# Layer kernel of a two-layer diffusion backbone: modulation loads issued from the GpSimd queue, and the last down weights of each FFN split once for two token blocks

## The chip, the cores and the metric

The kernel runs on one core of a Trainium2 chip. The metric is the device time of one execution in microseconds (us). Before the change it is 2483.01 us, the median of three runs (2481.47 to 2483.67).

Engines are named as in the profile: PE (TensorE matmuls; PEld is its weight load), DVE (VectorE), ACT (ScalarE), POOL (GpSimd) and SP (SyncE, which here only issues transfers). Each engine works through its own instructions in the order in which they stand. DMA transfers are issued by instructions on such a queue: "SPq" is the SP queue, and POOL's transfers stand in the same queue as POOL's arithmetic.

## The reference, cut to what matters

Two layers work on 512 latent tokens and 256 context tokens, all in float32:

```python
sh1, sc1, g1, sh2, sc2, g2 = split(silu(c) @ w_ada[l] + b_ada[l], 6)     # the modulation, once per layer
h = rmsnorm(x, norm1_g[l]) * (1 + sc1) + sh1
x = x + g1 * hybrid_mixer(h, hc, ...)     # three token mixers, merged by gates, then w_out
h = rmsnorm(x, norm2_g[l]) * (1 + sc2) + sh2
x = x + g2 * ((silu(h @ w_gate) * (h @ w_up)) @ w_down)
```

The context tokens go through the same in layer 0 (modulated by a constant vector), and only serve as keys and values in layer 1. w_ada has 1024 x 6144 elements a layer, w_gate and w_up 1024 x 2816, w_down 2816 x 1024.

## The kernel before, in words

Activations lie transposed, with features on the 128 partitions and tokens along the free dimension (768 tokens in layer 0, 512 in layer 1). Every dense product is done to float32 accuracy by three matmuls: a weight tile and an activation are each split into a high and a low part, and high x high, high x low and low x high are summed in PSUM.

**Weights.** `dense` (L303) computes one tile of 128 output features. `load_w` (L290) first loads the weight tile from HBM through the SP queue into one of three raw buffers `wr` (L283), copies it into the high part `wh` on ACT (L295), and subtracts to get the low part `wl` on DVE (L296); `wh` and `wl` have two buffers each. The matmuls of `dense` are at L313. A list `self.early` holds weights that were split ahead; `dense` takes from it first. In layer 0, most of the FFN's gate and up products use a seven-product scheme instead (`seven`, L419): POOL forms sums of weight blocks there (L435, four adds for each product of two tiles), which are split by ACT and DVE (L760, L761) and used by the matmuls at L413.

**Modulation.** The vector product with w_ada is not done on PE, apart from the first four units: its rows are multiplied in on DVE, a row of 128 x 512 weights at a time. `ada_load` (L545) loads one such row block `wra` (256 KB) into a pool with a single buffer, `aw`. `ada_step` (L549) multiplies it by a scalar per partition and adds it to an accumulator `acc` (L531 on DVE; the first row of each unit on ACT, L529). Where the modulation of latent and context tokens is needed (nb = 2), each row costs two such operations, otherwise one. `fill` (L609) does one step and issues the next load. `fill` is called after the tiles of the branch merge in `layer`, after the down tiles of the FFN pieces, and after each seven-product in layer 0. Since there is one buffer, the load of a row can't start before the operation on the row ahead of it has ended, and that operation stands in DVE's order between the weight splits (L296) and the other work. 136 row blocks go through `ada_load`; 24 more are loaded in pairs by `fill_unit` (L620) through the raw buffers.

**The FFN's last piece.** The FFN is cut into pieces of D_FF (`FF_PIECES`); each piece is followed by its part of the down product over eight tiles of output features, added to the residual stream X (`add_res`, L808). In the last piece the down product is done in two token blocks one after the other (layer 0: 512 latent and 256 context tokens; layer 1: 256 and 256), so that the norm of the first block (`settle`) can go on beside the second. Each block calls `dense` for all eight tiles, so each down tile of the last piece is loaded and split twice: 128 x 512 elements a tile in layer 0 (four blocks of D_FF), 128 x 768 in layer 1 (six).

**Pages.** Other tiles lie in 27 pages of two halves, taken (`pair`, `single`) and freed in the order of the program; a new tile in a page waits for the readers of the old one.

**Order.** The code is written in one order, and a scheduler places the instructions of each engine when the program is built. In layer 0's merge it stands up to three modulation rows to a tile of the merge, in layer 1's two. POOL's other work there is the sum `macc` (L1326), one add per merge tile, and the reload of X from its spill in HBM (L778).

Of the kernel before, what the change touches and what calls it, by code (L numbers as in the profile page):

```python
# [10 lines left out]
F32R = mybir.dt.float32r  # L11
# [5 lines left out]
P = 128  # L17
# [89 lines left out]
class Builder:  # L107
# [178 lines left out]
    def stationary(self, kt):  # L286
        return [pool.tile([P, KD, P], F32R, tag=tag, name=self.nm(tag))[:, 0:kt, :]
                for pool, tag in ((self.wh, "wh"), (self.wl, "wl"))]

    def load_w(self, wap, kt):  # L290
        nc = self.nc
        raw = self.load_raw(wap, kt)
        hi, lo = self.stationary(kt)
        r, h, o = (t.rearrange("p k c -> p (k c)") for t in (raw, hi, lo))
        nc.scalar.activation(out=h, in_=r, func=AF.Copy)  # L295
        nc.vector.tensor_tensor(out=o, in0=r, in1=h.bitcast(F32), op=ALU.subtract)  # L296
        return hi, lo
# [246 lines left out]

    def ada_load(self):  # L545
        self.ada_raw = self.aw.tile([P, 1, 512], F32, tag="aw", name=self.nm("wra"))
        self.nc.sync.dma_start(out=self.ada_raw, in_=self.ada_rows_of(1))

    def ada_step(self, w):  # L549
        state, l, units, nb, i, k = self.ada_queue.pop(0)  # L550
# [704 lines left out]
    def layer(self, l):  # L1255
        nc, a = self.nc, self.a
# [4 lines left out]
        def wcol(c0):  # L1261
            return win[:, c0:c0 + P]
# [40 lines left out]
        for bi, (idx, src) in enumerate(((2, cc), (0, at), (1, o))):  # L1303
# [5 lines left out]
            for m in range(KD):  # L1309
                pg = self.dense(wcol(OFF_GT + idx * D + m * P), act, [(0, tt)])  # L1310
# [35 lines left out]
        for bi, blk in enumerate(blocks):  # L1346
            for m in range(KD):
                ps = self.dense(a["w_out"][l][:, m * P:(m + 1) * P], mact, [blk[1:]])
# [8 lines left out]
        f0 = 0  # L1357
# [3 lines left out]
        for pi, n in enumerate(pieces):  # L1361
            last = pi == len(pieces) - 1
            gu, guheld = [], []
            for i in range(min(n, max(0, plain - f0))):
                c0 = (f0 + i) * P
                early = pi == 0 and i == 0
                rr = [blk[1:] for blk in blocks] if early else [(0, tt)]
                pg = self.dense(a["w_ffn_gate"][l][:, c0:c0 + P], act2, rr, outer=early)
                s = self.single("silu")
                nc.scalar.activation(out=s[:, 0:tt], in_=pg[:, 0:tt], func=AF.Silu)  # L1370
                pu = self.dense(a["w_ffn_up"][l][:, c0:c0 + P], act2, rr, outer=early)
                nc.vector.tensor_tensor(out=s[:, 0:tt], in0=pu[:, 0:tt], in1=s[:, 0:tt], op=ALU.mult)
                if i % 2 == 0:
                    hp, lp = self.pair("guh", F32R), self.pair("gul", F32R)
                    guheld += [hp, lp]
                self.split(s[:, 0:tt], hp[:, i % 2, 0:tt], lp[:, i % 2, 0:tt])
                self.free(s)
                gu.append((hp[:, i % 2, :], lp[:, i % 2, :]))
                if l == 0 and i > 0:
                    next(making)  # L1380
                    if i > 1:
                        next(making)
            if l == 0 and f0 + n == plain:
                quarters, qheld = next(making)
            elif l == 0:
                self.seven_gate_up(l, range(max(f0, plain), f0 + n, 2), quarters, gu, guheld)
            if last:
                self.free(*hheld)
                if l == 0:
                    self.free(*qheld)  # L1390
            if last and l == 0:
                self.norm_begin(1, ("n1g", 1, 2), 0, 1, "h")
            after = self.norm_shared if l == 0 else self.final_part
            for bi, blk in enumerate(blocks if last else [(None, 0, tt)]):
                for m in range(KD):
                    ps = self.dense(a["w_ffn_down"][l][f0 * P:(f0 + n) * P, m * P:(m + 1) * P], gu, [blk[1:]])
                    for bb in ([blk] if last else blocks):
                        self.add_res(m, ps, lambda b, m: self.mod[l][:, 40 + m, b:b + 1], bb)
                    if n > 2:
                        self.fill()  # L1400
                if last and bi == 0:
                    self.drain()
                self.finish_chains()
                if last and (l == 0 or bi == 0):
                    self.start_settle(blk, after, 0.0 if bi else PACE[1], l == 0)
            self.free(*guheld)
            f0 += n
# [125 lines left out]
```

## Time and profile before

| | |
|---|---|
| median of three runs | 2483.01 us |
| the profiled execution, its own time | 2482.72 us |
| its span, first to last instruction | 2480.9 us |
| mean granted TensorE clock | 0.993 |
| PE busy | 2397.0 us, 97% |
| DVE / ACT / POOL busy | 1555.1 / 900.3 / 308.9 us |

The profile is one execution of the program on the chip. In a group of instructions stand its line and engine, the tile that it writes and those it reads, the count, then busy time, the mean time of one, and the idle time of the engine ahead of them with what ended it. In a row of the waits stand the total wait, how often, and the longest. In a timeline row stand the start, the duration and the instruction, and in brackets the idle time ahead of it and its releaser. In the windows a stretch is followed by its length and by each engine's busy time and count.

### The profile page before, as it was taken

What the parts mean: (1) busy time and instruction counts of PE and PEld (TensorE: products, weight loads), DVE (VectorE), ACT (ScalarE), POOL (GpSimd) and SP (SyncE); (2) the same over time, 40 slices, a digit from 0 to 9 for tenths busy, and PEclk for the clock granted to TensorE, in tenths of its full rate; (3) what the DMA queues carried; (4) which work ended last, traced back from release to release, by engine and by line L of the source; (5) the groups of instructions that cost most, each with busy time, mean ns of one, the idle gap of its engine ahead of it and who ended that gap; (6) DMA issues with size and microseconds to landing.
All of it is one profiled execution on the core that took longest, in us unless ns stands there. A gap on an engine that the chain in (4) does not pass through costs nothing. (4 is left out here: it accounts for less than half of the span.)

```text
span 2480.9 us, 34528 instructions
## 1 busy us (share of the span) xinstructions
PE 2397.0 (97%) x13606; PEld 2083.7 (84%) x13606; DVE 1555.1 (63%) x2644; ACT 900.3 (36%) x1508; POOL 308.9 (12%) x215
## 2 busy tenths in 40 slices
PE   8999999999999999999999989999999999999998
PEld 3888888888788888889999978888887779888888
DVE  4688777875544366767666676678885457434335
ACT  3333344442122243233433453335453235322224
POOL 0000100000111120222232331000000112000001
PEclk9999999999999999999999999999999999999999
DMA  8222111123442241333343341111215455233334
GB/s 295 70 77 81 48 43 35 39 64 112 142 133 73 78 118 43 115 111 110 95 127 111 107 144 52 43 43 52 60 44 152 124 151 168 79 106 100 91 103 130
DMA packets 370673, 240.02 MB, mean 97 GB/s; under 512 B 9744, under 2 KB 341968, under 8 KB 370512
## 3 DMA queue, kind: packets, MB, share of 16 engines
q1 hardware_dynamic: 366576, 225.24, 30.6%
q0 software_dynamic: 2304, 10.49, 1.2%
q8 instruction: 107, 1.75, 0.3%
q10 hardware_dynamic: 1632, 2.10, 0.2%
q14 instruction: 54, 0.44, 0.1%
HBM read 230.45 MB, written 7.34 MB: 96 GB/s over the span
## 5 line engine op out<-in xcount | busy, mean ns | idle before, releaser
L295 ACT ACTIVATE wh<-wr 128x1024 fp32r<-128x1024 f32 (+4 forms) x344 | 308.0, 895 | 853.1 <-PE pd L313 727.2
L313 PE MATMUL pd<-hh,wl 128*128 128x512 f32 (+1 forms) x1504 | 451.9, 356 | 21.5 <-DVE wl L296 21.4
L296 DVE TENSOR_TENSOR wl<-wr,wh 128x1024 fp32r<-128x1024 f32 (+4 forms) x344 | 354.9, 1032 | 186.8 <-ACT wh L295 184.1
L313 PE MATMUL pd<-hh,wh 128*128 128x512 f32 (+1 forms) x1504 | 459.9, 362 | 0.7 <-ACT wh L295 0.6
L313 PE MATMUL pd<-hl,wh 128*128 128x512 f32 (+1 forms) x1504 | 446.7, 354 | 0.0
L313 PEld LDWEIGHTS pd<-hh,wl 128*128 128x128 f32 x1504 | 249.0, 190 | 65.7 <-DVE wl L296 28.9
L531 DVE SCALAR_TENSOR_TENSOR acc<-wra,sc,acc 128x512 f32<-128x512 f32 x224 | 169.6, 778 | 186.7 <-DMA wra<-in_w_ada 175.6
L313 PEld LDWEIGHTS pd<-hl,wh 128*128 128x128 f32 x1504 | 248.2, 190 | 34.4
L313 PEld LDWEIGHTS pd<-hh,wh 128*128 128x128 f32 x1504 | 249.7, 191 | 31.4 <-ACT wh L295 1.0
L313 PE MATMUL pd<-fh,wl 128*128 128x512 f32 (+1 forms) x496 | 175.3, 370 | 0.3 <-DVE wl L296 0.3
L313 PE MATMUL pd<-fl,wh 128*128 128x512 f32 (+1 forms) x496 | 175.7, 370 | 0.0
L313 PE MATMUL pd<-fh,wh 128*128 128x512 f32 (+1 forms) x496 | 174.4, 369 | 0.6 <-ACT silu L1370 0.6
L313 PE MATMUL pd<-guh,wh 128*128 128x512 f32 (+1 forms) x576 | 172.6, 341 | 1.8 <-ACT guh L760 0.9
L313 PE MATMUL pd<-guh,wl 128*128 128x512 f32 (+1 forms) x576 | 172.5, 340 | 1.8 <-DVE wl L296 1.8
L313 PE MATMUL pd<-gul,wh 128*128 128x512 f32 (+1 forms) x576 | 172.9, 340 | 0.1
L808 DVE SCALAR_TENSOR_TENSOR X<-pd,mod,X 128x256 f32<-128x256 f32 (+1 forms) x160 | 84.1, 560 | 85.3 <-PE pd L313 84.9
L313 PEld LDWEIGHTS pd<-guh,wh 128*128 128x128 f32 x576 | 98.3, 188 | 15.4 <-ACT guh L760 1.2
L313 PEld LDWEIGHTS pd<-guh,wl 128*128 128x128 f32 x576 | 98.6, 189 | 15.1 <-DVE wl L296 2.6
L313 PEld LDWEIGHTS pd<-gul,wh 128*128 128x128 f32 x576 | 98.7, 189 | 13.4 <-DVE gul L761 0.9
L313 PEld LDWEIGHTS pd<-fh,wl 128*128 128x128 f32 x496 | 90.1, 188 | 17.4 <-DVE wl L296 1.2
L313 PEld LDWEIGHTS pd<-fh,wh 128*128 128x128 f32 x496 | 89.5, 188 | 16.8 <-ACT silu L1370 0.8
L313 PEld LDWEIGHTS pd<-fl,wh 128*128 128x128 f32 x496 | 90.0, 188 | 15.5
(285 smaller groups left out, 4432.9 us busy)
## 6 DMA issues: line engine op xcount, KB each, us to landing
wr<-in_w_in SPq DMA_DIRECT2D x116, 512.0 KB, 3.9
wra<-in_w_ada SPq DMA_DIRECT2D x136, 256.0 KB, 2.8
wr<-in_w_ffn_gate SPq DMA_DIRECT2D x44, 512.0 KB, 3.9
wr<-in_w_ffn_up SPq DMA_DIRECT2D x44, 512.0 KB, 3.9
wr<-in_w_out SPq DMA_DIRECT2D x32, 512.0 KB, 3.7
wr<-in_w_branch SPq DMA_DIRECT2D x48, 256.0 KB, 3.0
wr<-in_w_ffn_down SPq DMA_DIRECT2D x48, 256.0 KB, 2.8
wr<-in_w_ffn_down SPq DMA_DIRECT2D x24, 384.0 KB, 3.3
```

Source lines behind the costliest of these rows:

```text
L295: nc.scalar.activation(out=h, in_=r, func=AF.Copy)
L296: nc.vector.tensor_tensor(out=o, in0=r, in1=h.bitcast(F32), op=ALU.subtract)
L313: nc.tensor.matmul(ps[:, b0:b1], lhsT=w[:, k, :], rhs=x[:, b0:b1], start=b not in first, stop=(k == kt - 1 and i == 2), skip_group_check=True)
L531: nc.vector.scalar_tensor_tensor(out=acc[:, 0:512], in0=w, scalar=sc, in1=acc[:, 0:512], op0=ALU.mult, op1=ALU.add)
L808: self.nc.vector.scalar_tensor_tensor(out=self.X[m][:, c0:c1], in0=ps[:, c0:c1], scalar=gcol(b, m), in1=self.X[m][:, c0:c1], op0=ALU.mult, ...
```

## The change

Two things are changed. `ada_load` issues its transfer from POOL's queue in place of SP's. And in the last piece of each FFN the eight down tiles are split in the first token block into pages (`keep_w`, one page pair `wk` for the high and low part of a tile), handed to `dense` through `self.early`, kept, used again in the second block, and freed there. The raw load through `wr` on SP stays for the first block; the loads and splits of the second block are gone. The splits into pages stand at L767 (ACT) and L768 (DVE) of the changed file, whose lines are 7 higher from `load_w` on.

```diff
+    def keep_w(self, wap, kt):
+        pg = self.pair("wk", F32R)
+        hi, lo = pg[:, 0, 0:kt * P], pg[:, 1, 0:kt * P]
+        self.split(self.load_raw(wap, kt).rearrange("p k c -> p (k c)"), hi, lo)
+        return pg, tuple(t.rearrange("p (k c) -> p k c", c=P) for t in (hi, lo))
...
     def ada_load(self):
         self.ada_raw = self.aw.tile([P, 1, 512], F32, tag="aw", name=self.nm("wra"))
-        self.nc.sync.dma_start(out=self.ada_raw, in_=self.ada_rows_of(1))
+        self.nc.gpsimd.dma_start(out=self.ada_raw, in_=self.ada_rows_of(1))
...
+            kept = []
             for bi, blk in enumerate(blocks if last else [(None, 0, tt)]):
                 for m in range(KD):
-                    ps = self.dense(a["w_ffn_down"][l][f0 * P:(f0 + n) * P, m * P:(m + 1) * P], gu, [blk[1:]])
+                    wap = a["w_ffn_down"][l][f0 * P:(f0 + n) * P, m * P:(m + 1) * P]
+                    if last:
+                        if bi == 0:
+                            kept.append(self.keep_w(wap, n))
+                        self.early.append(kept[m][1])
+                    ps = self.dense(wap, gu, [blk[1:]])
+                    if last and bi == 1:
+                        self.free(kept[m][0])
```

POOL's queue at the last seven-product of layer 0's FFN, before the change (the adds at L435 form the block sums of the up weights; `s` is the sum, `wr` the raw weights):

```order
L435 TENSOR_TENSOR s_1973_12352<-s_1973_12352,wr_12346 128x512
L435 TENSOR_TENSOR s_1974_12353<-s_1973_12352,wr_12346 128x512
L435 TENSOR_TENSOR s_1992_12482<-wr_12478 128x512
L435 TENSOR_TENSOR s_1993_12483<-wr_12476,wr_12478 128x512
L435 TENSOR_TENSOR s_1992_12482<-s_1992_12482,wr_12476 128x512
L435 TENSOR_TENSOR s_1993_12483<-s_1992_12482,wr_12476 128x512
```

The same place after it (L442 is the line L435 of before, L554 the transfer of `ada_load`):

```order
L442 TENSOR_TENSOR s_1974_12353<-s_1973_12352,wr_12346 128x512
L554 DMA wra_12474<-in_w_ada 128x512
L554 DMA wra_12603<-in_w_ada 128x512
L442 TENSOR_TENSOR s_1992_12482<-wr_12478 128x512
L442 TENSOR_TENSOR s_1993_12483<-wr_12476,wr_12478 128x512
L442 TENSOR_TENSOR s_1992_12482<-s_1992_12482,wr_12476 128x512
L554 DMA wra_12632<-in_w_ada 128x512
L442 TENSOR_TENSOR s_1993_12483<-s_1992_12482,wr_12476 128x512
L554 DMA wra_12654<-in_w_ada 128x512
```

The row loads now stand between the adds, and adds and loads wait for each other in the queue's order. In layer 0's merge the rows stand the same way between the `macc` adds, three to an add; and one row load moved to the very front of POOL's queue, ahead of the two instructions that complete the identity matrix.

DVE's order at the second token block of layer 0's last piece, before the change (X is the residual stream, 256 wide for the context tokens; `nt` and `hl` belong to the norm of the first block):

```order
L808 SCALAR_TENSOR_TENSOR X_6771<-pd_12849,mod_141,X_6771 128x256
L296 TENSOR_TENSOR wl_12900<-wr_12897,wh_12899 128x512
L721 SCALAR_TENSOR_TENSOR nt_12916<-X_6771,A_12611,rsb_12885 128x512
L808 SCALAR_TENSOR_TENSOR X_6772<-pd_12878,mod_141,X_6772 128x256
L296 TENSOR_TENSOR wl_12927<-wr_12924,wh_12926 128x512
L731 SCALAR_TENSOR_TENSOR hl_12915<-nt_12916,mod_142,hh_12914 128x512
L808 SCALAR_TENSOR_TENSOR X_6772<-pd_12903,mod_141,X_6772 128x256
```

And after it:

```order
L815 SCALAR_TENSOR_TENSOR X_6771<-pd_12829,mod_141,X_6771 128x256
L728 SCALAR_TENSOR_TENSOR nt_12884<-X_6771,A_12611,rsb_12859 128x512
L815 SCALAR_TENSOR_TENSOR X_6772<-pd_12852,mod_141,X_6772 128x256
L728 SCALAR_TENSOR_TENSOR nt_12903<-X_6771,A_12611,rsb_12859 128x512
L738 SCALAR_TENSOR_TENSOR hl_12883<-nt_12884,mod_142,hh_12882 128x512
L815 SCALAR_TENSOR_TENSOR X_6772<-pd_12871,mod_141,X_6772 128x256
```

The weight splits are gone from between the norm's steps; they stand ahead of the first block, and the first two weight tiles of the next layer are split inside the first block in place of behind the second.

## The prediction

> **What bounds the kernel now.** I read the page first, then the windows by stage, then the waits and timelines inside the stages that hold the changed instructions.
>
> ```profile
> span 2480.9 us, 34528 instructions
> PE 2397.0 (97%) x13606; PEld 2083.7 (84%) x13606; DVE 1555.1 (63%) x2644; ACT 900.3 (36%) x1508; POOL 308.9 (12%) x215
> L531 DVE SCALAR_TENSOR_TENSOR acc<-wra,sc,acc 128x512 f32<-128x512 f32 x224 | 169.6, 778 | 186.7 <-DMA wra<-in_w_ada 175.6
> ```
>
> PE is the bound, and only 84 us of the span has no matmul. DVE has slack as a whole, yet stands still for 175.6 us waiting for row loads of the modulation. Since DVE works in order, such a wait also holds up the weight split behind it. Where that reaches PE, the windows show (first the layer 0 merge, then three stretches of the layer 0 FFN with its end, the layer 1 merge, and two stretches with full PE for the pace):
>
> ```profile
> core 0: us, PE busy (x) PEld busy (x) DVE busy (x) ACT busy (x) POOL busy (x), PEclk, DMA share, GB/s
> 527.00:735.00 208.00, 197.92 (x1117) 170.98 (x1116) 117.40 (x194) 53.55 (x80) 15.26 (x10) 0.98 0.42 126
> 990.00:1070.00 80.00, 73.87 (x411) 65.85 (x410) 59.80 (x87) 22.70 (x36) 12.81 (x8) 1.00 0.36 107
> 1130.00:1210.00 80.00, 79.93 (x463) 75.31 (x462) 57.35 (x87) 27.64 (x41) 19.57 (x13) 1.00 0.37 110
> 1420.00:1480.00 60.00, 53.46 (x289) 45.60 (x288) 46.13 (x78) 31.62 (x53) 21.58 (x20) 0.97 0.52 153
> 1875.00:2050.00 175.00, 167.58 (x721) 135.26 (x720) 84.08 (x107) 52.89 (x76) 26.92 (x18) 0.99 0.50 148
> 2170.00:2232.00 62.00, 62.00 (x275) 51.36 (x274) 23.72 (x32) 16.24 (x20) 0.00 (x0) 1.00 0.36 106
> 2436.00:2452.00 16.00, 16.00 (x132) 15.70 (x132) 12.90 (x24) 8.24 (x15) 5.76 (x5) 1.00 0.58 173
> ```
>
> PE loses 10.1 us in the layer 0 merge, 7.4 in the layer 1 merge, 6.5 at the end of layer 0. A matmul of 512 columns takes 62.00/275 = 0.225 us, one of 256 columns 16.00/132 = 0.121. So a merge tile (36 matmuls of each width in layer 0) is 12.5 us of PE, in layer 1 (36 of 512) 8.1 us, and a down tile of a four-block piece in layer 0 (12 of each) 4.16 us.
>
> The chain of the rows in the layer 0 merge, DVE first, then SP:
>
> ```profile
> 574.69 1.41 DVE L531 SCALAR_TENSOR_TENSOR acc<-wra,sc,acc 128x512 f32<-128x512 f32 x2 [3.46 <-DMA wra<-in_w_ada]
> 576.02 1.22 DVE L296 TENSOR_TENSOR wl<-wr,wh 128x1024 fp32r<-128x1024 f32 x1
> 578.99 1.42 DVE L531 SCALAR_TENSOR_TENSOR acc<-wra,sc,acc 128x512 f32<-128x512 f32 x2 [1.75 <-DMA wra<-in_w_ada]
> 583.29 1.41 DVE L531 SCALAR_TENSOR_TENSOR acc<-wra,sc,acc 128x512 f32<-128x512 f32 x2 [1.13 <-DMA wra<-in_w_ada]
> ...
> 576.13 0.33 SPq L547 DMA_DIRECT2D wra<-in_w_ada  x1
> 580.43 0.33 SPq L547 DMA_DIRECT2D wra<-in_w_ada  x1
> ```
>
> DVE ends a row at 580.41, SP issues the next load at 580.43, and the next row starts at 583.29. The rows come every 4.30 us, all of it round trip: 1.41 us of work and 2.88 of waiting. Three rows a tile are 12.9 us against PE's 12.5, so this stage is already paced by that round trip; the FFN's down tiles hold one row each, 4.30 against 4.16. SP adds next to nothing, and its blocked weight loads don't reach PE: the L313 matmuls wait for splits, not for loads. So freeing SP buys little; what counts is the round trip through POOL.
>
> **The change part by part.**
>
> *The new round trip.* The trace has POOL transfers of other sizes (the reload of X and its spill) beside SP's rows of the same table:
>
> ```profile
> wra<-in_w_ada SPq DMA_DIRECT2D x136, 256.0 KB, 2.8
> wra<-in_w_ada SPq DMA_DIRECT2D x12, 512.0 KB, 3.7
> xd<-X POOLq DMA_DIRECT2D x4, 512.0 KB, 3.8
> X<-xd POOLq DMA_DIRECT2D x4, 512.0 KB, 4.9
> ```
>
> ```profile
> 1429.88 0.75 DVE L808 SCALAR_TENSOR_TENSOR X<-pd,mod,X 128x512 f32<-128x512 f32 x1 [0.48 <-PE pd L313]
> 1430.67 0.64 ACT L678 ACTIVATE sq<-X 128x512 f32<-128x512 f32 x1 [0.33 <-DVE X L808]
> 1430.93 0.72 POOL L772 DMA_DIRECT2D xd<-X  x1 [25.60 <-DVE X L808]
> ```
>
> At 512 KB POOL's transfers land 0.1 to 1.2 us after SP's do. And POOL starts one 0.30 us after DVE's operation has ended (1430.63 to 1430.93), where SP needed 0.02. So a row's round trip grows by 0.3 + (0.1 to 1.2), 0.4 to 1.5 us. I take 0.6: the loads of 4.9 were issued beside weight loads, so the store is the nearer row. Nothing excludes that a small POOL transfer lands faster than SP's, so the lower bound of the range is kept at no loss. [...]
>
> *Layer 0 merge.* About 15 tiles carry 42 rows, 2.8 a tile (the order keeps this). 2.8 x 4.90 = 13.7 us, and 0.3 for folding the accumulators, against 12.5: 1.5 us lost per tile, 22 in all, of which 10 are lost today: **+12**. POOL's `macc` add falls into the time in which a row's load is on its way, so it costs nothing; if it stood ahead of a due load it would cost its length.
>
> *Layer 0 FFN, row by row.* Two stretches of eight down tiles carry two-operation rows: 8 x (4.90 - 4.16) = 6 us, less the lead of about 3 us that DVE gains through two split buffers: +3 each. One-operation rows take 0.7 us less, 4.2, about PE's pace: +2 for three stretches. The rows among the first seven-products (990 to 1070, PE already 6 us idle): 8 x 0.6, +4 with a little hidden. Together **+12**. The cover is that lead; without it the two stretches cost 12.
>
> *POOL's order in the FFN.* Here rows stand behind block sums, and sums behind rows:
>
> ```profile
> 1398.39 1.30 POOL L435 TENSOR_TENSOR s<-wr 128x512 f32<-128x512 f32 x1 [9.04 <-DMA wr<-in_w_ffn_up]
> 1399.65 2.27 POOL L435 TENSOR_TENSOR s<-wr,wr 128x512 f32<-128x512 f32 x1
> 1401.89 3.44 POOL L435 TENSOR_TENSOR s<-s,wr 128x512 f32<-128x512 f32 x2
> 1397.74 0.75 DVE L531 SCALAR_TENSOR_TENSOR acc<-wra,sc,acc 128x512 f32<-128x512 f32 x1
> 1401.53 0.95 DVE L531 SCALAR_TENSOR_TENSOR acc<-wra,sc,acc 128x512 f32<-128x512 f32 x1 [0.76 <-DMA wra<-in_w_ada]
> ```
>
> By the new order the load of the row used at 1401.53 comes behind three of these four adds, to about 1403.6 in place of 1398.5: DVE is held 5 us, and behind that row stand splits and SiLU steps of the last seven-product. Two more places (around 1018 and 1265) have a row behind a block of 6 us or a block behind a row. I take 4, 2 and 2: **+8**, from 0 (all hidden in the lead) to 13.
>
> *Layer 1 merge.* Two one-operation rows a tile:
>
> ```profile
> 1890.79 4.75 DMA wra<-in_w_ada
> ...
> 1896.41 2.83 DMA wra<-in_w_ada
> ```
>
> The slow loads here come behind weights on the same queue: with 0.75 us for the operation such a row takes 5.5 us, the other kind 3.6, together 9.1 to a tile of 8.1. On a queue of its own a load may still share the engines with the weights. Two rows at 0.75 + 0.3 + 3.2 are 8.5 us: 0.4 lost a tile, 8 in the 21 tiles of the 175 us, where 7.4 are lost today, of which I leave 2 to 3 to other causes: **+3**, from -5 to +15.
>
> *The last pieces.* Sixteen loads, ACT copies and DVE subtractions go: 8 of 128x512 and 8 of 128x768. In layer 0's second block PE needs 12 x 0.121 = 1.45 us a tile, while DVE has a split, an add and the norm of the first block:
>
> ```profile
> L296 DVE TENSOR_TENSOR wl<-wr,wh 128x512 fp32r<-128x512 f32 x7 | 6.2, 881 | 1.1 <-ACT wh L295 1.1
> PE pd L313 <- DVE wl L296: 5.1, 4, 3.3
> ```
>
> The first row (1448 to 1466) shows the splits, 6.2 us, the second the waits of PE for them from 1438 to 1480, 5.1 us. These waits go, the longest because the next layer's first tiles are split earlier; the norm's chain is late next: **-6**, from -9 to -1 (the eight early splits stand ahead of the last gate-up steps and may delay the first block). In layer 1 the windows show PE full there: 0. The row load now first in POOL's queue adds 256 KB to the crowded start: **+1**.
>
> *Sum.* 12 + 12 + 8 + 3 - 6 + 1 = +30. On the profiled execution's 2482.7 us that is 2512.7, on the median 2483.0 (0.3 above it) **2513**.
>
> **The rivals.**
>
> A, *no longer round trip*: if POOL's small transfers land 0.3 us sooner than SP's, the cycle stays at 4.3, the merge rows gain from a queue without weights ahead (-4 in layer 0, -4 in layer 1), and the last pieces give 6: 2483 - 13 = **2470**. It decides from a landing below 2.6 us. For it speaks that the store of 512 KB is level with SP's load; against it the 4.9. [...] Chance 0.19.
>
> B, *POOL's queue is far slower*: rows land after 4 us as the 4.9 rows suggest, cycle 5.6. The merge alone is then 2.8 x 5.6 - 12.5 = 3.2 a tile, +38; the FFN +35, the layer 1 merge +20: **2570**. Chance 0.08.
>
> C, *hidden anyway*: the longer trip is eaten by DVE's lead and by contention that ends, and only about 6 come and 6 go: **2483**. Against it: the merge has three rows at 4.3 to a tile of 12.5, no lead survives 15 tiles of that. Chance 0.11.
>
> **How the numbers follow.** My forecast has 0.62, 2513. Its range alone goes with 0.3 to 0.95 us on the round trip and the bounds above, 2490 to 2550. With rivals A and C the range is 2472 to 2552, leaving out about half of A and most of B. A measurement of this kernel can tell a difference of about 0.2%, 5 us, from none. Faster by more than that: A, 0.19. Within: C, 0.11. Slower: the forecast and B, 0.70.
>
> **What would show it.** Right, if the landing of the POOL row loads is 3.0 to 3.6 us, rows in the layer 0 merge come every 4.8 to 5.0 us, PE's idle time there is about 22 us, DVE's total wait for rows is above 230 us, and PE's wait from 1438 to 1480 for splits is gone. Wrong, if rows come every 4.4 us or less, or if the merge's idle time falls below 10 us.

## The result, and the profile after

The changed kernel takes 2539.26 us (median of four runs, 2535.46 to 2540.7) against 2482.24 us before: the ratio is 1.0229, with a 95% interval from 1.0211 to 1.0247. The profiled execution took 2535.46 us, 52.7 more than that of before. Forecast were 2513 us, a range of 2472 to 2552, and slower as the likeliest.

From the page of the profile after, the span, the busy times and the group of the row operations (L538 is L531 of before):

```profile
span 2533.4 us, 34395 instructions
PE 2411.7 (95%) x13606; PEld 2093.0 (83%) x13606; DVE 1539.2 (61%) x2628; ACT 890.6 (35%) x1492; POOL 376.8 (15%) x351
L538 DVE SCALAR_TENSOR_TENSOR acc<-wra,sc,acc 128x512 f32<-128x512 f32 x224 | 166.5, 765 | 259.8 <-DMA wra<-in_w_ada 252.9
```

DVE waits for rows 252.9 us, where it waited 175.6. The span grew by 52.5 us, and this is not only idle time of PE: the same 13606 matmuls are busy 14.7 us longer, and 37.8 us are idle.

The windows by stage show where. The limits in the trace after are put at the same matmuls as those of before, counted in PE's order, so that a row and its counterpart hold the same work to within one matmul. Before (the layer 0 merge with what follows up to the FFN, the FFN, the end of its last piece, the attention of layer 1, its merge, the rest):

```profile
527.00:945.00 418.00, 403.17 (x2285) 349.85 (x2284) 228.43 (x337) 123.13 (x173) 55.65 (x32) 0.99 0.36 107
945.00:1441.40 496.40, 484.41 (x2727) 449.78 (x2725) 326.37 (x459) 174.15 (x263) 116.88 (x78) 1.00 0.36 106
1441.40:1499.50 58.10, 51.56 (x301) 44.54 (x301) 44.13 (x75) 31.63 (x52) 16.79 (x15) 0.97 0.44 125
1499.50:1860.50 361.00, 351.14 (x2121) 301.32 (x2120) 269.83 (x540) 150.91 (x300) 27.14 (x18) 1.00 0.17 48
1860.50:2057.70 197.20, 189.68 (x850) 154.17 (x849) 100.91 (x139) 65.54 (x99) 29.01 (x20) 0.99 0.48 143
2057.70:2480.90 423.20, 414.51 (x2193) 357.02 (x2191) 195.96 (x301) 142.11 (x209) 26.70 (x24) 1.00 0.37 110
```

And after:

```profile
526.70:962.40 435.70, 409.93 (x2285) 354.23 (x2284) 228.57 (x337) 123.26 (x173) 81.88 (x80) 0.97 0.35 103
962.40:1495.60 533.20, 496.90 (x2727) 457.99 (x2726) 329.07 (x462) 176.67 (x265) 145.41 (x134) 0.97 0.35 102
1495.60:1544.30 48.70, 48.24 (x300) 42.73 (x300) 32.18 (x64) 24.71 (x42) 16.21 (x15) 1.00 0.20 62
1544.30:1904.80 360.50, 351.10 (x2120) 301.32 (x2120) 272.00 (x540) 150.88 (x300) 26.89 (x18) 1.00 0.17 48
1904.80:2109.00 204.20, 191.50 (x851) 155.19 (x849) 99.78 (x139) 65.37 (x99) 45.70 (x51) 0.98 0.47 138
2109.00:2533.40 424.40, 414.35 (x2192) 357.13 (x2191) 188.49 (x293) 136.81 (x201) 23.37 (x24) 1.00 0.35 102
```

By stage that is +17.7, +36.8, -9.4, -0.5, +7.0 and +1.2, together 52.8; the first of these matmuls comes 0.3 us sooner than before. The layer 0 FFN is the largest loss: the 2727 matmuls are busy 496.90 us, 12.5 longer, at a granted clock of 0.97 in place of 1.00. The end of the last piece is the one clear gain.

The chain of a row in the layer 0 merge, in the timelines of DVE and POOL, and the row loads in the page's list of transfers:

```profile
595.39 1.41 DVE L538 SCALAR_TENSOR_TENSOR acc<-wra,sc,acc 128x512 f32<-128x512 f32 x2 [2.40 <-DMA wra<-in_w_ada]
600.32 1.41 DVE L538 SCALAR_TENSOR_TENSOR acc<-wra,sc,acc 128x512 f32<-128x512 f32 x2 [2.05 <-DMA wra<-in_w_ada]
...
597.10 0.54 POOL L554 DMA_DIRECT2D wra<-in_w_ada  x1 [4.41 <-DVE acc L538]
602.03 0.54 POOL L554 DMA_DIRECT2D wra<-in_w_ada  x1 [4.39 <-DVE acc L538]
...
wra<-in_w_ada POOLq DMA_DIRECT2D x136, 256.0 KB, 3.2
```

DVE ends at 596.80, POOL issues at 597.10, the next row starts at 600.32, 4.93 us after the one ahead of it: 1.41 for the two operations, 0.30 for the start, 3.2 for the landing, as against 4.30 before.

What a stall does to the clock is seen in windows of 2 us around the longest one, where PE waits 7 us for a split:

```profile
1308.00:1310.00 2.00, 0.64 (x4) 0.32 (x2) 0.83 (x2) 1.06 (x1) 0.00 (x0) 1.00 0.49 150
1310.00:1312.00 2.00, 0.00 (x0) 0.00 (x0) 2.00 (x3) 0.00 (x0) 1.76 (x3) 0.92 0.26 66
1312.00:1314.00 2.00, 0.00 (x0) 0.00 (x0) 2.00 (x1) 0.00 (x0) 2.00 (x3) 0.50 0.17 66
1314.00:1316.00 2.00, 0.38 (x1) 0.38 (x2) 2.00 (x3) 0.00 (x0) 1.92 (x2) 0.50 0.47 131
1316.00:1318.00 2.00, 2.00 (x7) 2.00 (x7) 1.79 (x2) 0.52 (x1) 0.70 (x1) 0.50 0.00 0
1318.00:1320.00 2.00, 2.00 (x11) 2.00 (x11) 0.00 (x0) 0.48 (x1) 0.00 (x0) 0.87 0.00 0
1320.00:1322.00 2.00, 2.00 (x14) 2.00 (x13) 0.37 (x1) 1.00 (x2) 0.00 (x0) 1.00 0.00 0
```

From 1316 to 1318 PE is never idle, yet does 7 matmuls where it does 14 from 1320: the granted clock is 0.50. Counted in such windows from 500 to 2300 us, there are 6 stretches of halved clock before and 14 after; the busy time lost in them, the sum of busy time times (1 - clock), is 9.8 us before and 25.2 after. The difference of 15.4 is close to the 14.7 us by which the page has PE busier.

### The profile page after: what moved, and what is told of

Same layout as the page of the kernel before. It is cut to its first block, busy times and chain, and to the rows that moved or that the text cites. A ratio compares the mean times of both kernels' runs of the same rounds, so it can differ in the third digit from the quotient of the medians.

```text
span 2533.4 us, 34395 instructions
## 1 busy us (share of the span) xinstructions
PE 2411.7 (95%) x13606; PEld 2093.0 (83%) x13606; DVE 1539.2 (61%) x2628; ACT 890.6 (35%) x1492; POOL 376.8 (15%) x351
## 5 line engine op out<-in xcount | busy, mean ns | idle before, releaser
L302 ACT ACTIVATE wh<-wr 128x1024 fp32r<-128x1024 f32 (+4 forms) x312 | 284.4, 912 | 821.8 <-PE pd L320 701.4
L303 DVE TENSOR_TENSOR wl<-wr,wh 128x1024 fp32r<-128x1024 f32 (+4 forms) x312 | 329.3, 1056 | 180.9 <-ACT wh L302 178.3
L538 DVE SCALAR_TENSOR_TENSOR acc<-wra,sc,acc 128x512 f32<-128x512 f32 x224 | 166.5, 765 | 259.8 <-DMA wra<-in_w_ada 252.9
L554 POOL DMA_DIRECT2D wra<-in_w_ada x136 | 74.2, 546 | 677.7 <-DVE acc L538 439.2
L320 PE MATMUL pd<-guh,wh 128*128 128x512 f32 (+1 forms) x416 | 123.9, 355 | 4.0 <-ACT guh L767 3.0
L320 PE MATMUL pd<-gul,wh 128*128 128x512 f32 (+1 forms) x416 | 125.6, 358 | 1.8 <-DVE gul L768 1.7
L320 PE MATMUL pd<-guh,wl 128*128 128x512 f32 (+1 forms) x416 | 124.1, 355 | 0.0
L687 POOL TENSOR_TENSOR sqa<-sqa,sq 128x256 f32<-128x256 f32 (+1 forms) x40 | 47.9, 1197 | 415.6 <-ACT sq L685 412.5
L320 PEld LDWEIGHTS pd<-fl,wh 128*128 128x128 f32 x496 | 90.0, 188 | 15.8
L320 PE MATMUL pd<-brh,wh 128*128 128x512 f32 (+1 forms) x288 | 87.0, 356 | 0.0
```

The costliest lines, as they stand in the source:

```text
L320: nc.tensor.matmul(ps[:, b0:b1], lhsT=w[:, k, :], rhs=x[:, b0:b1], start=b not in first, stop=(k == kt - 1 and i == 2), skip_group_check=True)
L538: nc.vector.scalar_tensor_tensor(out=acc[:, 0:512], in0=w, scalar=sc, in1=acc[:, 0:512], op0=ALU.mult, op1=ALU.add)
L554: self.nc.gpsimd.dma_start(out=self.ada_raw, in_=self.ada_rows_of(1))
L687: eng.tensor_tensor(out=acc[:, c0:c1], in0=acc[:, c0:c1], in1=sq[:, c0:c1], op=ALU.add)
```

## The experiments

Four theories are used below. **R**: each row costs its longer round trip, which the order of the program lets through to PE. **O**: loads and block sums hold each other up in POOL's queue. **K**: the kept down tiles cost time. **S**: the software queue itself (the pages list POOL's as q0 software_dynamic, with 5.9% of the 16 DMA engines' span after and 1.2% before) costs something beyond its longer way. A fifth, **P**, came up on the way and is told at e9.

For each run the table gives the ratio to the kernel before with its interval, the shortest distance between two two-operation rows in the layer 0 merge ("cycle"), and what each stage took beyond that of before, between the same matmuls of the two traces (merge 0: 527.7 to 766.6 us of before; FFN 0: 945.0 to 1441.4; end 0: to 1499.5; merge 1: 1860.5 to 2057.7). A stage is read from one traced execution of each kernel; e1 and e11, whose programs are alike in merge 1, differ there by 2.7 us, so differences of 2 or 3 us between stages say little.

| run | median, ratio [interval] | cycle | merge 0 | FFN 0 | end 0 | merge 1 |
|---|---|---|---|---|---|---|
| before | 2482 to 2486 | 4.23 | 0 | 0 | 0 | 0 |
| after | 2539.3, 1.0229 [1.0211, 1.0247] | 4.80 | 17.7 | 36.7 | -9.3 | 7.0 |
| e1 | 2544.5, 1.0245 [1.023, 1.026] | 4.76 | 19.5 | 31.3 | -0.5 | 9.3 |
| e2 | 2480.4, 0.9978 [0.997, 0.9987] | | 0.7 | 1.7 | -9.4 | 4.8 |
| e3 | 2470.5, 0.9948 [0.9933, 0.9962] | | -10.1 | 3.9 | -9.2 | 0.7 |
| e4 | 2485.0, 1.0003 [0.9994, 1.0012] | | -7.9 | 5.5 | -9.4 | 3.9 |
| e5 | 2513.2, 1.0116 [1.0103, 1.0129] | 4.82 | 20.2 | 0.6 | 1.2 | 9.3 |
| e6 | 2503.4, 1.0077 [1.0064, 1.009] | 4.42 | 7.0 | 11.9 | 1.0 | -0.1 |
| e7 | 2487.4, 1.0008 [0.9999, 1.0018] | 4.25 | 2.2 | 0.7 | -1.0 | 4.0 |
| e8 | 2470.4, 0.9945 [0.9933, 0.9958] | | -9.0 | 2.3 | -9.2 | -0.4 |
| e9 | 2511.5, 1.0111 [1.0095, 1.0126] | 4.87 | 9.0 | 22.0 | 1.0 | -5.3 |
| e10 | 2491.1, 1.0034 [1.0021, 1.0047] | 4.91 | -3.3 | 15.8 | -0.6 | -3.1 |
| e11 | 2535.8, 1.0209 [1.0195, 1.0223] | 4.83 | 18.9 | 23.4 | 1.8 | 12.0 |
| e12 | 2576.7, 1.0365 [1.0351, 1.0379] | 5.39 | 26.8 | 44.8 | 1.1 | 14.9 |

**e1, the queue alone** (the kernel before with this line):

```diff
-        self.nc.sync.dma_start(out=self.ada_raw, in_=self.ada_rows_of(1))
+        self.nc.gpsimd.dma_start(out=self.ada_raw, in_=self.ada_rows_of(1))
```

> The kernel before with the row loads on POOL's queue and nothing else. Theory R (the whole loss is the row loads' way through POOL; the kept down tiles bring about 10 us at the end of layer 0): 2483 + 57 + 10 = 2550 us (2540 to 2560), with the same losses as after up to the last piece: about 16 us in the layer 0 merge, 37 in its FFN, 7 in the layer 1 merge. Theory K (the kept tiles, by splitting eight tiles ahead of the last steps and by holding pages, cause a good part of the loss): below 2525 us.

Measured 2544.5: the queue alone costs 60 us, more than both edits together. Theory K falls.

**e2, the kept tiles alone** (the kernel after with e1's line turned back).

> The kernel after with the row loads back on SP's queue. Theory R: 2483 - 8 = 2475 us (2468 to 2480), the gain all between 1420 and 1480 us, nothing elsewhere. Theory K: 2490 us or more, PE losing time ahead of the last piece and about 3 us in the last piece of layer 1.

Measured 2480.4, 0.22% faster, 5 us short of R's number and 10 better than K's least. The end of layer 0 gives 9.4 us as expected. Against it stand 4.8 us in the layer 1 merge, and 3.1 in the last gate-up steps of layer 1; R had neither, K had the second. The waits of PE there (2380 to 2445 us of e2) show about half of the latter:

```profile
PE pd L320 <- ACT guh L767: 1.6, 1, 1.6
```

In before, PE waits for nothing at that place. The eight new splits stand ahead of the last activation's split on ACT. The 4.8 us go with another placing of the rows: before, four tiles in the middle of the layer 1 merge carry no row; with the kept tiles the rows run on through them. That link was not tried by itself.

**e3 and e4, two loads under way** (e2 and after, with a second buffer; the row loads alternate between the pool and a half page):

```diff
-            self.ada_step(self.ada_raw[:, 0, :])
-            self.ada_raw = None
-            if self.ada_queue:
-                self.ada_load()
+            pg, v = self.ada_raws.pop(0)
+            self.ada_step(v)
+            if pg is not None:
+                self.free(pg)
+            while len(self.ada_raws) < min(2, len(self.ada_queue)):
+                self.ada_load(len(self.ada_raws))
```

> As e2 (SP's queue, kept tiles), and two row loads under way at a time (the second buffer is a half page). If a row's round trip, one load after the other, is what paces DVE (theory R), the merges' idle time goes too: 2475 - 30 = 2445 us (2435 to 2460), and DVE waits under 60 us for rows. If the row waits cost PE nothing of themselves and POOL's order is the cause (theory O), 2475 us, as e2.

> As after (POOL's queue, kept tiles), and two row loads under way at a time. Theory R: a longer round trip no longer counts, since the next row is there already: 2450 us (2440 to 2475), about as e3. Theory O (loads and POOL's adds holding each other up in POOL's order): the adds in the layer 0 FFN still stand among the loads, so some 15 to 35 us remain over e3: 2465 to 2490 us, all of it between 950 and 1450 us.

With two loads under way POOL's queue costs 14.6 us over SP's (2485.0 against 2470.5), where with one it cost 58.9 (2539.3 against 2480.4): three quarters of the loss hang on the chain of load, operation, load. The 14.6 us are at the low end of what O had for e4 over e3, but not in O's place: the FFN differs by 1.6 us between the two runs, so the order alone, without the chain, is nearly free there. Where R was wrong is the size of the gain. In e3 DVE's waits for rows fall to this:

```profile
DVE acc L538 <- DMA wra<-in_w_ada: 53.1, 36, 6.0
```

They fall by 122 us against before, and the time by 13.5, of which the kept tiles have 3.6. Most of those waits never reached PE; and the freed rows now stand in clumps of up to five or six in a tile's share of DVE's order.

**e5, POOL's queue in the merges only** (the kernel before, with a flag that the merge loop sets):

```diff
+        (self.nc.gpsimd if self.ada_merge else self.nc.sync).dma_start(out=self.ada_raw, in_=self.ada_rows_of(1))
```

> The kernel before with the row loads on POOL's queue in the two merges only, on SP's in the FFN; no kept tiles. Theory R (each stage pays for its own longer round trips): 17 us in the layer 0 merge and 8 in layer 1's, 2484 + 25 = 2509 us (2502 to 2515), the FFN as before. If the merge's rows, by ending later, shift the rest (theory shift), part of the FFN's 34 us comes too: 2520 us or more.

Measured 2513.2, 28 us over before: 20.2 and 9.3 in the two merges, 0.6 in the FFN. Each stage pays for its own rows, and nothing is carried on.

**e6 and e9, a longer trip on SP's queue** (the kernel before; e6 the first line, e9 the second):

```diff
+        self.nc.gpsimd.memset(self.ada_raw[0:1, 0, 0:1], 0.0)
...
+        self.nc.gpsimd.memset(self.ada_raw[:, 0, :], 0.0)
...
         self.nc.sync.dma_start(out=self.ada_raw, in_=self.ada_rows_of(1))
```

> The kernel before, the row loads still on SP's queue, but each waits for a one-element memset of its buffer on POOL: the round trip is longer by POOL's start and the handover, and POOL's order is that of e1, with no software queue. I estimate a row's cycle of 4.7 to 4.9 us in the layer 0 merge. Theory R and theory O: most of e1's loss, 2520 to 2545 us. Theory S (the software queue itself, its descriptors or its packets beside DVE, is what costs): under 2505 us.

Measured 2503.4. The cycle grew by only 0.19 to 0.25 us, since POOL starts a memset 0.11 us after DVE's operation, where it starts a transfer after 0.30. From e6's timelines of DVE and POOL:

```profile
580.42 1.42 DVE L531 SCALAR_TENSOR_TENSOR acc<-wra,sc,acc 128x512 f32<-128x512 f32 x2 [2.17 <-DMA wra<-in_w_ada]
...
581.95 0.09 POOL L547 MEMSET wra<- 1x1 f32 x1 [4.63 <-DVE acc L531]
```

The number fell on theory S's side, but the dose was smaller than expected, and by dose it speaks for R: the medians of the cycle are about 4.36 (before), 4.61 (e6) and 5.01 (e1); that is 0.25 and 0.65, a ratio of 0.38. The losses of e6 and e1 are 7.0 and 19.5 in the merge, 11.9 and 31.3 in the FFN, ratios of 0.36 and 0.38. DVE's order in the layer 0 merge, counted in row operations to a tile, is the same in both. If the loss goes in proportion to the cycle, that leaves theory S nothing to explain there. Nor do the pages of before and e1 show a price elsewhere: the weights on SP's queue land after the same time (3.9 and 3.8 us for w_in, 3.9 and 3.9 for w_up, 2.8 and 2.8 for w_down).

> As e6, with a memset of the whole row buffer (128x512) in place of one element, so that POOL holds each row up longer: I estimate 0.5 us for it and a cycle of 5.0 us in the layer 0 merge, that of e1, still with SP's hardware queue. Theory R with POOL's order: as much as e1, 2484 + 60 = 2544 us (2530 to 2555). Theory S (the software queue costs something beyond its longer way): 2484 + 20 to 40, under 2525 us.

Measured 2511.5, and this missed R by 33 us: at a cycle as long as e1's the merge lost 9.0 in place of 19.5. The order gives a reason. These are the row operations between successive outputs of the merge on DVE (two to a row; a unit's first row runs on ACT and is not counted), for the first 20 tiles; e6 has e1's row:

```
before  6 4 6 6 4 6 6 4 6 4 6 6 4 6 4 2 0 0 0 0
e1      6 4 6 6 4 6 6 2 6 6 4 6 4 6 4 4 0 0 0 0
e9      6 4 5 5 4 4 6 4 4 5 4 1 6 6 2 5 5 4 0 0
e10     5 4 2 6 4 4 4 6 4 4 4 6 2 6 4 2 6 4 4 0
e12     5 6 3 5 4 4 5 5 3 5 5 3 4 6 4 4 4 6 0 0
```

With the memset the scheduler spread the rows over 18 tiles in place of 16, presumably because it counts the memset's time (0.53 us in e9's trace). For the transfer on POOL's queue it left the rows packed up to three to a tile, as for the short trip. So what costs in this merge would be rows to a tile times the cycle, and not the cycle alone: theory P.

**e10, the longer trip through ACT** (as e9, with a copy on ACT in place of the memset):

```diff
+        self.nc.scalar.copy(out=self.ada_raw[:, 0, 0:448], in_=cap(self.ones, 0, [[0, 448]]))
```

> As e9, but the row buffer is first written by a 128x448 copy on ACT, so POOL's order has no part. I estimate 0.6 us for it. Theory R (the cycle alone): the layer 0 merge loses 15 to 18 us as in e1, and the FFN 12 to 20 in place of 33; 2484 + 35 = 2519 us (2510 to 2530). If POOL's order is nothing, as e9.

Measured 2491.1, under R's range. The FFN's 15.8 us came as expected (12 to 20); the merge, with rows spread over 19 tiles, even gains 3.3. The shortest cycle is longer than e1's, and the whole loss is 6.6 us where e1's is 60: the cycle alone does not set the price. The layer 1 merge gains 5.3 us in e9 and 3.1 in e10. The transfers there, of before (1880 to 2050) and of e9 (1915 to 2080):

```profile
wra<-in_w_ada SPq DMA_DIRECT2D x29, 256.0 KB, 3.5
...
PE pd L313 <- DVE wl L296: 7.3, 6, 3.0
```

```profile
wra<-in_w_ada SPq DMA_DIRECT2D x30, 256.0 KB, 3.0
...
PE pd L313 <- DVE wl L296: 3.0, 2, 2.8
```

Issued half a microsecond later, the rows land after 3.0 us in place of 3.5, and PE's waits there fall from 7.3 to 3.0 us. I take it that they then miss the weights ahead of them on SP's queue; no run moved the weights instead.

**e7, ACT's queue** (e1's line with `nc.scalar`).

> The kernel before with the row loads on ACT's queue. The landing is that of SP's, 2.8 us; the start after DVE's operation about 0.3 us later, so a cycle of 4.6 us. Theory R: half of e1's loss, 2510 us (2500 to 2525), with POOL's adds free. If ACT's order holds the loads up (its splits and activations wait for PE), rows are late by up to a whole tile: 2550 us or more.

Measured 2487.4, level with before to 0.1%. Both guesses were wrong: ACT's issue adds nothing to the shortest cycle (4.25 against 4.23), and the order had the rows spread, so that ACT's own work did not hold them up.

**e8, the best of these** (e3 with the kept tiles in layer 0 only: `if last and l == 0`).

> As e3 (SP's queue, two row loads under way), with the kept tiles in layer 0's last piece only. The 2 to 3 us that layer 1's last gate-up steps lost behind eight early splits come back: 2470.5 - 2.5 = 2468 us (2464 to 2471). If those 2 to 3 us have another cause, 2470 us, as e3.

Measured 2470.4, level with e3; the last gate-up steps of layer 1, 1.5 us longer than before in e3, are as before in its trace, but the time doesn't show it. It is 0.55% faster than before, and 2.7% faster than after.

**e11, loads kept clear of the block sums** (e1, with 30 of the 136 loads back on SP):

```diff
+        (self.nc.sync if self.ada_seven else self.nc.gpsimd).dma_start(out=self.ada_raw, in_=self.ada_rows_of(1))
...
+                self.ada_seven = True
                 self.fill()
+                self.ada_seven = False
...
+                        self.ada_seven = l == 0 and m >= KD - 3
                         self.fill()
+                        self.ada_seven = False
```

> As e1, but in layer 0's FFN the loads that stood among or next to the block sums (issued at the seven-products and at the last three down tiles of a piece) go through SP's queue; the other loads stay on POOL's. Theory O (loads and block sums hold each other up, at three places): the FFN's loss falls from 33 to about 10 us, 2544 - 23 = 2521 us (2514 to 2528). Theory R alone: only some 24 rows lose their 0.65 us, 2544 - 8 = 2536 us.

Measured 2535.8, R's number: the FFN loses 23.4 us in place of 31.3. At most some 8 us come from the neighbourhood of loads and block sums, the longer trips of those 30 rows among them.

**e12, a still longer trip** (e9's memset, then e1's transfer).

> As e1 (row loads on POOL's queue, no kept tiles), with e9's memset of the row buffer ahead of each load, so that the round trip is longer still: I estimate a cycle of 5.5 us in the layer 0 merge. The order built for it spreads the rows over 18 merge tiles, 2.25 to a tile (e9: 2.15, e1: 2.56 over 16). Theory P (the loss is rows to a tile times the cycle, and e1 loses because its order packs rows as for the short trip): the layer 0 merge loses 2.25 x 5.5 = 12.4 against 12.5, so no more than e1's 17 us, I take 8 to 15; the FFN about as e1, 25 to 40; together 2484 + 50 = 2534 us (2520 to 2552). Theory R (each row costs its longer trip, whatever the order): 0.5 us more on every row than e1, 2570 us or more, the layer 0 merge losing over 30.

Measured 2576.7: R's number, and P's price fails by 40 us. The merge's 26.8 lies between the two. Against e9, whose rows are spread much alike, 0.5 us more of cycle costs 65 us in all; and before against e1, packed much alike, 0.6 us costs 60. For a given order the cycle costs as R has it. e1 and e9, at one cycle, differ by 33 us: 10.5 in the layer 0 merge, where the table of row operations shows another order, 9.3 in the FFN, and 14.6 in the layer 1 merge, where the order of the rows is the same but for one and P explains nothing. Both steps along the cycle, and that from e1 to e9, also change the queue, so that these three runs by themselves don't part R and P from S; the pair e6 and e1 does, in the layer 0 merge and the FFN.

## Why the prediction held, and where it was too small

The result lies in the range, and the direction was right, but the loss of 57 us is nearly twice the forecast 30. The terms were sums of PE's idle time, and as such most of them came out near their size; what the sum left out is that PE also runs slower after many of its stalls, at a granted clock of 0.50 in 14 stretches of after. That the range still holds the result is partly luck, since its bounds were set for the round trip and had no such term.

**The round trip** was right. Rows were to land after 3.0 to 3.6 us and to come every 4.8 to 5.0; they land after 3.2 and come every 4.80 at the shortest, 4.99 in the median. POOL's start was 0.30, and the landing, 3.2 in place of the 2.8 on SP's queue before, is 0.4 us longer.

**The layer 0 merge**, +12. In the working's own stretch (before 527 to 735 us) after takes this:

```profile
526.90:747.50 220.60, 202.59 (x1115) 174.12 (x1114) 115.02 (x189) 53.63 (x80) 38.45 (x53) 0.96 0.39 117
```

That is +12.6, the forecast number, but made up otherwise: PE is idle 18.0 us in place of the 22 forecast, and 4.7 us of the loss are longer busy time. So the number itself is in part luck. By the start of the FFN the loss is 17.7, 10.9 of it idle and 6.8 busy. That rows packed to a tile set the pace was right for the order that was built; e9 and e10 show what a looser packing costs.

**The FFN**, +12 for the rows and +8 for POOL's order: +36.8, of which 24.3 are idle, against the 20 of the working, and 12.5 longer busy time, against nothing. The runs part the two terms roughly: e1 has 19.5 us more idle time there than before, and e11, with its loads clear of the sums, 13.4. So in idle time the rows were near their 12, and POOL's order near its 8. The lead of 3 us, which the working counted as cover, was not tried by itself. One of the two places named there, from 1265 us of before, became the worst stall of the kernel. From the timelines of POOL and DVE after:

```profile
1300.96 3.98 POOL L442 TENSOR_TENSOR s<-s,wr 128x512 f32<-128x512 f32 x2
1304.89 0.56 POOL L554 DMA_DIRECT2D wra<-in_w_ada  x1
...
1309.17 0.75 DVE L538 SCALAR_TENSOR_TENSOR acc<-wra,sc,acc 128x512 f32<-128x512 f32 x1 [5.38 <-DMA wra<-in_w_ada]
1309.84 1.14 DVE L815 SCALAR_TENSOR_TENSOR X<-pd,mod,X 128x512 f32<-128x512 f32 x2
1310.89 4.67 DVE L768 TENSOR_TENSOR wl<-s,wh 128x1024 fp32r<-128x1024 f32 x1
```

The row that DVE had released at 1301.55 is loaded at 1304.89, behind the sums; DVE stands 5.38 us; and the split behind it takes 4.67 us beside POOL's next sums, where a split of this size takes 1.23 in the mean of the 200 at L303; the one at 1302.53 took 1.26 beside sums as well, so the sums alone are not shown to be the cause. PE waits 7 us and then runs at half clock (0.50 until 1318.5). That clearing such places gained so little in e11 is no contradiction: there another stall, of 5.8 us, took its place (the stretch from 1225 to 1350 us of before still loses 11.1, in place of e1's 14.1).

**The clock**, not in the sum at all: PE's 14.7 us of longer busy time, of the 52.5. Without them the loss is the 37.8 us by which the idle time grew, against a forecast of 30. By the trace's clock records each of the 14 halved stretches of after lasts 3.41 us or twice that, and their distances are multiples of it, so that they lie on one grid of 3.41 us. In the window of the grid ahead of each of them PE was busy 0.36 to 2.06 us, so in none was it idle throughout. Two windows of the grid around a stall of 3.3 us that ended at 698.9, and two around one of 1.4 us that ended at 915.3:

```profile
693.79:697.21 3.42, 1.85 (x11) 1.35 (x10) 0.90 (x2) 0.63 (x1) 0.00 (x0) 1.00 0.42 172
697.21:700.62 3.41, 1.70 (x9) 1.51 (x10) 1.65 (x2) 0.00 (x0) 0.54 (x1) 1.00 0.34 99
912.33:915.75 3.42, 2.06 (x18) 1.86 (x18) 1.47 (x3) 0.98 (x2) 1.96 (x1) 1.00 0.54 162
915.75:919.16 3.41, 3.41 (x18) 3.41 (x17) 1.41 (x2) 0.72 (x1) 0.00 (x0) 0.50 0.51 150
```

The longer stall lies across two windows, with PE busy 1.85 and 1.70 us in them, and the clock stayed at 1.00. The shorter lies in one, with PE busy 2.06 us, and the next window was at half clock. So neither the length of a stall nor PE's busy time in the window decides by itself here, and the exact condition stays open.

**The layer 1 merge**, +3: +7.0, of which 5.2 are idle. A queue of its own did bring the landing from 3.5 to 3.2 us, as the working had it, but the rows come every 4.4 us (the median there; 3.95 before), and two of them are 8.8 against PE's 8.1. That this is not the cause, or not all of it, is shown by e9 and e10: their rows come every 4.4 us too, on SP's queue, and they gain 5.3 and 3.1. The kept tiles are not needed for the loss: e1 loses 9.3.

**The last pieces**, -6: -9.4, with the waits for splits gone; from 1482 to 1525 us of after PE waits for this alone:

```profile
PE rsb L673 <- POOL rs L659: 0.4, 1, 0.4
```

The idle time fell by 6.1 us, the forecast number; the other 3.3 are shorter busy time, the granted clock being 1.00 in place of 0.97. For layer 1 the working had 0, with the cover of a full PE; from 2380 to 2442 us of before after takes 1.7 us more, where the eight splits stand.

**The start**, +1: the merge's first matmul came 0.3 us sooner, so this cost did not show.

**The rivals.** A (2470) needed a landing under 2.6 us, about SP's 2.8 less the 0.30 of POOL's start; 3.2 was measured. B (2570) needed rows that land after 4 us; the median is 3.2, though single rows took up to 5.7. C (2483) fell with the loss in the merge and the FFN.

What stays open: whether the software queue has a price of its own (in the layer 0 merge and FFN e6 and e1, by dose, leave little room for it; no run has e1's order and cycle on SP's queue; in the layer 1 merge, where after and e1 lose 7.0 and 9.3 on POOL's queue and e9 and e10 gain on SP's at the same cycle, it may), and why the layer 1 merge differs by 4 us between e2, e4 and e7 on one side and e3, e6 and e8 on the other.

## What to carry to other kernels

A load that waits for its own buffer is a chain, and its round trip counts once per link (here 4.93 us a row in place of 4.30): before it is moved to another queue, count the links that stand between two pieces of the bounding engine's work, and multiply. How tightly the order packs the links counts beside their length (at shortest cycles of 4.76 to 4.91 us e1, e9 and e10 lose 60, 27 and 7 us, with rows over 16, 18 and 19 tiles of the layer 0 merge, e1 on POOL's queue and the others on SP's); a second buffer (e3, e4) took away three quarters of the difference between the two queues (14.6 us in place of 58.9). When PE is the bound, add to the stalls what the halved clock costs afterwards, here 1 to 3 us for each of the 14 stretches of after; not every stall had one (that of 3.3 us at 698.9 did not).

## What was not expected of the hardware

- POOL starts an operation of its own 0.11 us after DVE releases it, but a transfer 0.30 us after (e6 and after); ACT's queue added nothing to the shortest cycle of a row (4.25 against 4.23, e7 and before).
- A stall can cost beyond its length: 14 stretches of halved clock (0.50) took 25.2 us in after, 1.8 each, and one of them followed a stall of only 1.4 us.
- A split of 128x1024 on DVE took 4.67 us in place of 1.23 beside sums on POOL (after, at 1310.89); another beside sums took 1.26 (at 1302.53).
- Loads issued half a microsecond later landed 0.5 us sooner (e9 in the layer 1 merge), and PE waited 3.0 us for splits there in place of 7.3.
